# PEER layer on one Trainium2 core: 64 of 256 tokens by gathered rows, 192 by dense products

## The chip, the core and the metric

The kernel runs on one core of a Trainium2 chip. The core has five engines that run their own instruction queues in order: TensorE for matrix products (in the profile PE, its weight loads apart as PEld), VectorE (DVE), ScalarE (ACT), GpSimd (POOL) and SyncE (SP), the last of which here only issues transfers. Transfers run on 16 DMA engines. The metric is the device time in microseconds (us) of one execution; lower is better.

## The reference

A two-layer block over 256 latent tokens and 256 context tokens, D = 1024. Each layer ends in a PEER step: for every token 8 heads choose 16 of 16384 experts each, so 128 experts a token, and every expert has a row in a table u and a row in a table v (1024 numbers each).

```python
def _peer(h, w_query, sub_keys, expert_u, expert_v):
    ...
    idx = jnp.take_along_axis(cand_idx..., pos, axis=-1)      # (token, head, 16)
    gate = jax.nn.softmax(best, axis=-1)
    def retrieve(args):
        hb, ib, gb = args
        act = jax.nn.gelu(jnp.einsum('td,thkd->thk', hb, expert_u[ib]), approximate=False)
        wgt = gb * act
        return jnp.einsum('thk,thkd->td', wgt, expert_v[ib])
    ...
# last layer: only the 256 latent tokens go through _peer, then
x = x + xg2 * _peer(hx, ...)
return rmsnorm(x, final_norm_w)
```

## The kernel before

The kernel is one long program; a scheduler orders each engine's queue when it is compiled. In the last layer PEER is done **dense**, for all 256 tokens at once, in these steps:

- `dense_select`: the normed tokens (transposed, split into two rounded parts `Hh` and `Hl`, so that products in the one-pass type fp32r keep their precision) are scored against the keys; `chosen` holds for each token the two key numbers and the gate of its 128 choices. VectorE does most of it.
- `build`: for every token VectorE makes two one-hot matrices (`two`, one instruction for 4 tokens, and `one`, one for each token), TensorE multiplies them into the token's 128x128 table of gates, ScalarE copies it out, and SP writes it to DRAM (`gd<-gs`), 16 tokens a transfer, 16 transfers.
- `stream`: a loop over the 128 row blocks of the tables, 128 experts each. `first(i)` loads the u block (`w<-in_tab`, 512 KB), splits it into `hu` (ScalarE) and `lu` (VectorE, line 1108), and does 24 products (lines 1118 to 1120): 8 slices of the contraction by three terms, u stationary 128x128, tokens moving, 256 columns; Gelu gives `we`. `second(i)` loads the gates of 8 blocks at a time (`g<-gd`, line 1127) and the v block (`hv`, `lv`), multiplies (line 1133), splits the weights into `wh`, `wl`, and does 12 products (line 1141): 2 token blocks by three terms by 2 halves, the weights stationary, v moving, 512 columns. They add up in the four banks `po`, `po`, `pj`, `pj` over all 128 blocks.
- `first` may run ahead of `second` by `LAG[1]` = 32 blocks. The first `second` needs the gates of all 256 tokens, that is, the end of `build`.
- `residual` scales the sums by a row and adds them to the tokens; then the final norm.

The first layer's context tokens go another way, which the change reuses: `gather_rows.by_choice` fetches for each of 128 choices the rows of u (one token on each partition, 4 KB each, 512 KB a fetch, an indirect DMA that POOL issues), and one VectorE instruction (line 982) makes the 128 dot products; then for each token the 128 rows of v are fetched, and TensorE sums them with weights in 32-column tiles (line 1005). Seven buffers (`ROWS`) hold fetched rows.

Of the kernel before, what the change touches and what calls it, by code (L numbers as in the profile page):

```python
# [8 lines left out]
F32 = mybir.dt.float32  # L9
# [86 lines left out]
def _layout(i):  # L96
# [25 lines left out]
    for l in range(depth):  # L122
        a[f"wmod{l}"] = _tiles(i["w_mod"][l], 512)
        w = i["w_in"][l]
        a[f"win{l}"] = _tiles(w[:, :1536], 256)
        a[f"wba{l}"] = np.ascontiguousarray(w[:, 1536:1552].reshape(KT, 128, 16).transpose(1, 0, 2))
        a[f"wrest{l}"] = _tiles(w[:, 1552:], 512)
        a[f"wout{l}"] = _tiles(i["w_out"][l], 512)
        a[f"wq{l}"] = _tiles(i["w_query"][l], 256)
        k = i["sub_keys"][l].reshape(16, 128, 128)  # L130
        a[f"keys{l}"] = np.ascontiguousarray(k.transpose(2, 0, 1))
        if l < depth - 1:
            a[f"u{l}"], a[f"v{l}"] = i["expert_u"][l], i["expert_v"][l]
# [12 lines left out]
def _body(st, tc, a, out, dbg, until):  # L146
# [16 lines left out]
    def nm(s):  # L163
        n_names[0] += 1
        return f"{s}_{n_names[0]}"
# [879 lines left out]
    AHEAD = 100000  # L1045
    HB = {"u": 2, "v": 2}

    def dense_select(l, s, m, dp, side):
# [15 lines left out]
        for b in range(NB):  # L1064
            p = bank([128, 3, 128], f"c{b}")
            for i in range(3):
                pe.transpose(p[:, i], sel[:, b, i].rearrange("p h k -> p (h k)"), ident)
            act.copy(chosen[:, :, b * 128 : b * 128 + 128], p)
        sp.close()
        return Hh, Hl, chosen  # L1070

    def build(chosen, gdram, side, banks):

        bp = Stage("build", side)
        for tg in range(T // TG):
            gs = bp("gs", [128, NKEYS, TG], 2)
            for t4 in range(0, TG, 4):
                t0 = tg * TG + t4
# [12 lines left out]
            nc.sync.dma_start(gdram[:, tg], gs)  # L1091
        bp.close()

    def stream(l, gdram, Hh, Hl, make_u, make_v, lag, between=()):

        acc = [[bank([128, 512], tag) for _ in range(2)] for tag in ("po", "pj")]
        scores = bank([128, 2, T], "s")
# [15 lines left out]
        def first(i):  # L1113
            hi, lo = table(i, 0, "u", dve.tensor_tensor, make_u)
            p = scores[:, i % 2]
            for k in range(KT):
                ks = slice(k * 128, k * 128 + 128)
                pe.matmul(p, hi[:, ks], Hh[:, k], start=(k == 0), stop=False)  # L1118
                pe.matmul(p, hi[:, ks], Hl[:, k], start=False, stop=False)  # L1119
                pe.matmul(p, lo[:, ks], Hh[:, k], start=False, stop=(k == KT - 1))  # L1120
            w = acts[i] = make_u("we", [128, T], lag + 1)
            act.activation(w, p, AF.Gelu)

        def second(i):
            if i % IG == 0:
                acts["g"] = make_v("g", [128, T // TG, IG, TG], 2)
# [5 lines left out]
            wh = make_v("wh", [128, T], 2, F32R)  # L1132
            dve.tensor_tensor(wt, wt, g, OP.mult)
            act.copy(wh, w)  # L1134
            wl = make_v("wl", [128, T], 2, F32R)
            dve.tensor_tensor(wl, w, wh.bitcast(F32), op=OP.subtract)
            for b in range(NB):
                ts = slice(b * 128, b * 128 + 128)
                for j, (x, y) in enumerate(((wh, hi), (wh, lo), (wl, hi))):
# [13 lines left out]
                second(i - lag)  # L1153
        return acc

    def gdram():
        return dr.tile([128, T // TG, NKEYS, TG], F32, tag="g", name=nm("gd"))


    m = mods[0]  # L1160
# [93 lines left out]
    su = Stage("stream_u", "right")  # L1254
    sw = Stage("split")
    with using(split=sw):
        Hh, Hl, keys = dense_select(1, LAT, m, dp, "right")
    sw.close()
    sv = Stage("stream_v")
    gd = gdram()  # L1260
    build(keys, gd, "right", ("c0", "c1", "c2"))
    residual(1, LAT, m, stream(1, gd, Hh, Hl, su, sv, LAG[1]))
    sv.close()
    su.close()
    dp.close()

# [26 lines left out]
```

## Time and profile before

| | us |
|---|---|
| median of 3 runs | 3301.32 (3293.26 to 3307.34) |
| the profiled execution, its own time | 3294.41 |
| its span, first to last instruction | 3292.7 |
| last layer: `build` runs in | 2495 to 2635 |
| last layer: first product of `second` | 2645.7 |
| last layer: products of `second` end | 3276.4 |

| engine | busy us | share of the span |
|---|---|---|
| PE | 2858.5 | 87% |
| PEld | 2348.9 | 71% |
| DVE | 2207.6 | 67% |
| ACT | 1343.1 | 41% |
| POOL | 860.7 | 26% |

Shares of the whole span mix stages with different limits, so the stages of the last layer are read one by one. Each view of the profile shows what an engine did in a stretch and, in square brackets, how long it had waited and for whom.

### The profile page before, as it was taken

To read this page: it belongs to the slowest core of one execution; us is meant where nothing else is said; L and a number is where in the kernel's file an instruction comes from. 1 tells how busy PE (TensorE), PEld (TensorE's weight loads), DVE (VectorE), ACT (ScalarE), POOL (GpSimd) and SP (SyncE) were. 2 spreads that over 40 slices of the span, in tenths; PEclk is the share of its full clock that TensorE was granted. 3 is DMA by queue.
4 is the path that set the end of the run, shared out by engine and by line. 5 is a ranking of instruction groups with operands and counts; after the bars stand their busy time and mean duration, and the time that the engine had idled before them with its cause. 6 is when DMAs were issued, how large, how long until landed. Compare 5 with 4: busy or idle time off the path is not lost. (4 is left out here: it accounts for less than half of the span.)

```text
span 3292.7 us, 47160 instructions
## 1 busy us (share of the span) xinstructions
PE 2858.5 (87%) x17467; PEld 2348.9 (71%) x17467; DVE 2207.6 (67%) x4920; ACT 1343.1 (41%) x2348; POOL 860.7 (26%) x638
## 2 busy tenths in 40 slices
PE   7998954778897888878789999999779889999998
PEld 4686744645452676767678999868578878889997
DVE  4534587789982688889895655652499955555555
ACT  4432212201251344444455645543335644544443
POOL 0140018985445333333310122134230000000000
PEclk8998976888899989999999999999889999999999
DMA  7622416589899999999985543361234575566663
GB/s 260 212 94 64 153 58 217 181 290 349 311 389 389 343 369 360 367 367 389 383 325 189 172 154 116 92 227 52 95 124 171 201 239 201 199 206 205 213 212 131
DMA packets 246165, 746.52 MB, mean 227 GB/s; under 512 B 21168, under 2 KB 94256, under 8 KB 225456
## 3 DMA queue, kind: packets, MB, share of 16 engines
q1 hardware_dynamic: 190320, 474.54, 41.8%
q0 software_dynamic: 55296, 268.46, 21.8%
q8 instruction: 137, 2.24, 0.3%
q14 instruction: 92, 0.75, 0.1%
q10 hardware_dynamic: 320, 0.52, 0.1%
HBM read 707.27 MB, written 35.65 MB: 226 GB/s over the span
## 5 line engine op out<-in xcount | busy, mean ns | idle before, releaser
L1118 PE MATMUL s<-Hh,hu 128*128 128x256 f32 x2048 | 601.5, 294 | 73.4 <-ACT hu L1107 50.5
L1120 PE MATMUL s<-Hh,lu 128*128 128x256 f32 x2048 | 599.5, 293 | 58.9 <-DVE lu L1108 58.9
L1119 PE MATMUL s<-Hl,hu 128*128 128x256 f32 x2048 | 592.2, 289 | 0.0
L1118 PEld LDWEIGHTS s<-Hh,hu 128*128 128x128 f32 x2048 | 404.7, 198 | 95.7 <-ACT hu L1107 58.2
L1108 DVE TENSOR_TENSOR lu<-w,hu 128x1024 fp32r<-128x1024 f32 x256 | 315.9, 1234 | 228.9 <-ACT hu L1107 228.8
L1120 PEld LDWEIGHTS s<-Hh,lu 128*128 128x128 f32 x2048 | 404.7, 198 | 72.1 <-DVE lu L1108 71.6
L1108 DVE TENSOR_TENSOR lv<-w,hv 128x1024 fp32r<-128x1024 f32 x256 | 314.9, 1230 | 173.3 <-ACT hv L1107 164.3
L1119 PEld LDWEIGHTS s<-Hl,hu 128*128 128x128 f32 x2048 | 405.0, 198 | 8.4
L1107 ACT CAST hu<-w 128x1024 fp32r<-128x1024 f32 x256 | 267.8, 1046 | 330.2 <-PE s L1119 253.0
L1107 ACT CAST hv<-w 128x1024 fp32r<-128x1024 f32 x256 | 267.4, 1044 | 159.8 <-PE pj L1141 116.1
L970 POOL DMA_INDIRECT uv<-in_uv,idx x128 | 206.9, 1616 | 405.1 <-DVE acc L1029 384.7
L982 DVE SCALAR_TENSOR_TENSOR uv<-uv,h 128x1024 f32<-128x1024 f32 x128 | 189.3, 1493 | 45.3 <-DMA uv<-in_u,idx 45.0
L232 POOL TENSOR_TENSOR C<-L,levels 128x512 f32<-128x512 f32 x96 | 137.8, 1446 | 290.4 <-DVE L L645 166.7
L970 POOL DMA_INDIRECT uv<-in_u,idx x128 | 177.6, 1387 | 45.3 <-issue 24.4
L1141 PE MATMUL po<-hv,wh 128*128 128x512 f32 x512 | 164.7, 402 | 14.3 <-ACT wh L1134 13.8
L970 POOL DMA_INDIRECT uv<-in_v,idx_t x128 | 131.1, 1024 | 129.1 <-PE s L1005 103.4
L1141 PE MATMUL po<-lv,wh 128*128 128x512 f32 x512 | 162.7, 399 | 0.1
L1141 PE MATMUL po<-hv,wl 128*128 128x512 f32 x512 | 162.2, 397 | 0.0
L1029 DVE SCALAR_TENSOR_TENSOR acc<-uv,dot,acc 128x1024 f32<-128x1024 f32 x127 | 162.2, 1277 | 0.0
L1141 PE MATMUL pj<-hv,wl 128*128 128x512 f32 x512 | 162.1, 397 | 0.0
L1141 PE MATMUL pj<-lv,wh 128*128 128x512 f32 x512 | 162.1, 396 | 0.0
L1141 PE MATMUL pj<-hv,wh 128*128 128x512 f32 x512 | 161.7, 397 | 0.0
(426 smaller groups left out, 5883.6 us busy)
## 6 DMA issues: line engine op xcount, KB each, us to landing
w<-in_tab SPq DMA_DIRECT2D x512, 512.0 KB, 4.6
w<-in_wmod SPq DMA_DIRECT2D x96, 512.0 KB, 4.7
gd<-gs SPq DMA_DIRECT2D x32, 1024.0 KB, 5.5
g<-gd SPq DMA_DIRECT2D x32, 1024.0 KB, 8.4
w<-in_wq SPq DMA_DIRECT2D x48, 512.0 KB, 4.0
w<-in_win SPq DMA_DIRECT2D x44, 512.0 KB, 4.2
w<-in_wrest SPq DMA_DIRECT2D x24, 512.0 KB, 3.7
w<-in_wout SPq DMA_DIRECT2D x24, 512.0 KB, 4.5
```

Source lines behind the costliest of these rows:

```text
L232: pool.tensor_tensor(out, x, y, op=op)
L970: pool.indirect_dma_start(out=t, out_offset=None, in_=a[f"{table}{l}"], in_offset=bass.IndirectOffsetOnAxis(ap=index, axis=0))
L982: dve.scalar_tensor_tensor(u, u, 1.0, st["h2", b], op0=OP.mult, op1=OP.mult, accum_out=dots[:, j : j + 1])
L1029: dve.scalar_tensor_tensor(acc, uv[:, D:], dot, acc, op0=OP.mult, op1=OP.add)
L1107: act.copy(hi, raw)
L1108: eng(lo, raw, hi.bitcast(F32), op=OP.subtract)
L1118: pe.matmul(p, hi[:, ks], Hh[:, k], start=(k == 0), stop=False)
L1119: pe.matmul(p, hi[:, ks], Hl[:, k], start=False, stop=False)
L1120: pe.matmul(p, lo[:, ks], Hh[:, k], start=False, stop=(k == KT - 1))
L1141: pe.matmul(acc[b][n], x[:, ts], y[:, n * 512 : n * 512 + 512], start=(i == 0 and j == 0), stop=(i == NKEYS - 1 and j == 2),)
```

## The change

In the last layer, tokens 192 to 255 (`FEW` = 64) leave the dense path. `dense_select` makes their expert numbers in two layouts, and their normed rows; the 128 partitions hold 64 tokens twice. `gather_few` does for them what `by_choice` does: 64 fetches of u (choice j of the 64 tokens and choice j + 64), 64 dot products on VectorE, and 64 fetches of v (one token each) with 32 steps of 4 products on TensorE. `build` and `stream` work on 192 tokens. In `second` the product is turned round: v is stationary (8 slices of 128 columns), the weights move (192 columns), 24 products in place of 12, and the sums come out transposed. So after the stream four copies, 16 transposes and two more copies bring them back to token order. In the diff the parts follow one another as they stand in the code: `dense_select`, `gather_few`, `build`, `first`, `second`, and the main part of the last layer.

```diff
+        if rows is not None:
+            ts = slice(T - FEW, T)
+            idx_f = sp("idx_f", [128, FEW])
+            dve.scalar_tensor_tensor(idx_f, chosen[:, 0, ts], float(NKEYS), chosen[:, 1, ts], op0=OP.mult, op1=OP.add)
...
+                pe.matmul(p[cs], idx_f, ident[:, cs], start=True, stop=True)
+            dve.tensor_copy(idx, p)
+            h2 = rows("h2", [128, D])
...
+    def gather_few(l, rows):
...
+        for j in range(FEW):
+            u = fetch("u", few["idx"][:, j : j + 1])
+            dve.scalar_tensor_tensor(u, u, 1.0, few["h2"], op0=OP.mult, op1=OP.mult, accum_out=dots[:, j : j + 1])
...
+        act.activation(w_t, p, AF.Gelu)
+        dve.tensor_tensor(w_t, w_t, few["gate"], OP.mult)
+        dve.tensor_copy(spots_of, w_t.rearrange("p (g r) -> p g r", g=2))
+        p = bank([128, 512], "vb")
+        for r in range(pairs):
+            vs = [fetch("v", few["idx_t"][:, g * pairs + r : g * pairs + r + 1]) for g in range(2)]
+            for n in range(2):
+                for g in range(2):
+                    o = 32 * (2 * n + g)
+                    pe.matmul(
+                        p[o : o + 32], wz[:, g * pairs + r], vs[g][:, n * 512 : n * 512 + 512],
+                        start=(r == 0), stop=(r == pairs - 1), tile_position=(0, o),
+                    )
...
-        for tg in range(T // TG):
+        for tg in range(n // TG):
...
-                pe.matmul(p, hi[:, ks], Hh[:, k], start=(k == 0), stop=False)
+                pe.matmul(p, hi[:, ks], Hh[:, k, 0:n_tok], start=(k == 0), stop=False)
...
+            terms = ((wh, hi), (wh, lo), (wl, hi))
+            if n_tok < T:
+                for k in range(KT):
+                    for j, (x, y) in enumerate(terms):
+                        pe.matmul(
+                            acc[k // 4][k // 2 % 2][:, k % 2 * n_tok : k % 2 * n_tok + n_tok],
+                            y[:, k * 128 : k * 128 + 128], x,
...
-    build(keys, gd, "right", ("c0", "c1", "c2"))
-    residual(1, LAT, m, stream(1, gd, Hh, Hl, su, sv, LAG[1]))
+    build(keys, gd, "right", ("c0", "c1"), n_tok)
+    with using(vb="c2"):
+        y = gather_few(1, rows)
+    sv = Stage("stream_v")
+    sums = stream(1, gd, Hh, Hl, su, sv, LAG[1], n_tok=n_tok)
+    yT = sv("yT", [128, KT, n_tok])
...
+            pe.transpose(ps[k // 4][0:n, k % 4 * 128 : k % 4 * 128 + 128], yT[:, k, b * 128 : b * 128 + n], ident)
...
+    residual(1, LAT, m, halves)
```

The scheduler puts the new work between the old. All queues are as before up to the last layer's selection. VectorE, in the middle of `build`, before: one-hot matrices (`two`, `one`) and the split of u blocks (`lu`).

```order
L1108 TENSOR_TENSOR lu_21794<-w_21791,hu_21793 128x1024
L1081 TENSOR_TENSOR two_20489<-chosen_19040,iota 128x512
L1088 TENSOR_SCALAR one_20491<-iota,chosen_19040 128x128 x4
L1081 TENSOR_TENSOR two_20502<-chosen_19040,iota 128x512
L1088 TENSOR_SCALAR one_20504<-iota,chosen_19040 128x128 x4
L1108 TENSOR_TENSOR lu_21826<-w_21823,hu_21825 128x1024
```

And now, at the same place: the dot products (`uv,dots`, line 1117) stand among them.

```order
L1151 TENSOR_TENSOR two_20504<-chosen_19040,iota 128x512
L1158 TENSOR_SCALAR one_20506<-iota,chosen_19040 128x128 x4
L1117 SCALAR_TENSOR_TENSOR uv_20972,dots_20899<-uv_20972,h_4293_20217 128x1024
L1117 SCALAR_TENSOR_TENSOR uv_20975,dots_20899<-uv_20975,h_4293_20217 128x1024
L1117 SCALAR_TENSOR_TENSOR uv_20978,dots_20899<-uv_20978,h_4293_20217 128x1024
L1117 SCALAR_TENSOR_TENSOR uv_20981,dots_20899<-uv_20981,h_4293_20217 128x1024
L1178 TENSOR_TENSOR lu_22011<-w_22008,hu_22010 128x1024
L1117 SCALAR_TENSOR_TENSOR uv_20984,dots_20899<-uv_20984,h_4293_20217 128x1024
L1151 TENSOR_TENSOR two_20519<-chosen_19040,iota 128x512
```

All 64 dot products stand between the first and the last of the 48 groups (one `two` and four `one`) that `build` now has; 21 `lu` stand there, where 22 stood before among 64 groups.

TensorE, in the stream: the products of a v step (`wz`, line 1132) now stand between those of `first` (lines 1188 to 1190). The product that needs only the first of the step's two fetches stands alone, the three others follow later in a row.

```order
L1188 MATMUL s_21367<-Hh_19035,hu_23068 128x192
L1132 MATMUL c_4524_21099<-uv_21270,wz_20897 32x512
L1132 MATMUL c_4524_21099<-uv_21268,wz_20897 32x512
L1132 MATMUL c_4524_21099<-uv_21270,wz_20897 32x512
L1189 MATMUL s_21367<-Hl_19036,hu_23068 128x192
L1190 MATMUL s_21367<-Hh_19035,lu_23069 128x192
```

Of the 128 products of the v steps 40 (10 steps) stand ahead of the first product of `second`, and 88 (22 steps) behind it, in 43 such runs. Ahead of it stand 34 blocks of `first`, before as now.

TensorE at the end of the stream, before: the last product of `first` stands 24 products ahead of the end of `second`.

```order
L1119 MATMUL s_21086<-Hl_19036,hu_27362 128x256
L1120 MATMUL s_21086<-Hh_19035,lu_27363 128x256
L1141 MATMUL po_21082<-hv_28115,wh_28119 128x512
L1141 MATMUL po_21083<-hv_28115,wh_28119 128x512
L1141 MATMUL po_21082<-lv_28116,wh_28119 128x512
```

And now it stands 337 products, 14 blocks of `second`, ahead of it.

```order
L1189 MATMUL s_21367<-Hl_19036,hu_28783 128x192
L1190 MATMUL s_21367<-Hh_19035,lu_28784 128x192
L1212 MATMUL pj_4594_21366<-wl_29458,hv_29451 128x192
L1212 MATMUL po_21363<-wh_29490,hv_29486 128x192
L1212 MATMUL po_21363<-wh_29490,lv_29487 128x192
```

In these names the operand in front is the one that moves, and the one behind it is stationary.

## Rows read from the trace of the kernel before

**Rows 1.** Windows: length; busy us (instructions) by engine; granted clock, DMA share, GB/s
```profile
2495.00:2635.00 140.00, 128.71 (x1053) 124.46 (x1054) 131.41 (x343) 91.07 (x110) 0.00 (x0) 1.00 0.57 200
2635.00:2646.00 11.00, 0.86 (x6) 0.67 (x6) 1.22 (x4) 1.59 (x4) 0.00 (x0) 0.65 0.79 244
2646.00:3276.00 630.00, 629.35 (x3791) 559.39 (x3791) 356.63 (x472) 299.92 (x439) 0.00 (x0) 1.00 0.61 203
3276.00:3293.00 17.00, 0.41 (x2) 0.00 (x0) 11.88 (x36) 2.30 (x4) 0.00 (x0) 0.62 0.23 93
```
**Rows 2.** Timeline of VectorE in `build`: start, us, engine, line, operation
```profile
2602.00 1.22 DVE L1108 TENSOR_TENSOR lu<-w,hu 128x1024 fp32r<-128x1024 f32 x1
2603.14 0.69 DVE L1081 TENSOR_TENSOR two<-chosen,iota 128x512 f32<-128x512 f32 x1
...
2604.76 0.68 DVE L1081 TENSOR_TENSOR two<-chosen,iota 128x512 f32<-128x512 f32 x1
```
**Rows 3.** Timeline from the end of `build` to the first product of `second`
```profile
2639.17 8.92 SPq L1127 DMA_DIRECT2D g<-gd  x3
2644.78 2.77 DVE L1133 TENSOR_TENSOR we<-we,g 128x256 f32<-128x256 f32 x8 [12.25 <-DMA g<-gd]
...
2645.69 1.22 PE L1141 MATMUL po<-hv,wh 128*128 128x512 f32 x2 [10.14 <-ACT wh L1134]
```
**Rows 4.** Timeline of TensorE in the stream: first product of three neighbouring blocks of products
```profile
2849.78 0.28 PE L1118 MATMUL s<-Hh,hu 128*128 128x256 f32 x1
...
2852.65 0.62 PE L1141 MATMUL po<-hv,wh 128*128 128x512 f32 x2
...
2855.43 0.63 PE L1141 MATMUL po<-hv,wh 128*128 128x512 f32 x2
```
**Rows 5.** Timeline of weight loads and products in runs: start, us of the whole run
```profile
2111.09 0.97 PEld L476 LDWEIGHTS s<-g,same 128*128 128x128 f32 x8
2111.20 0.96 PE L476 MATMUL s<-g,same 128*128 128x8 f32 x8
...
309.65 1.67 PE L256 MATMUL pj<-hT,w 128*128 128x256 f32 x7
```
**Rows 6.** Single loads (shortest/median/longest ns); products of line 256 (busy us, mean ns)
```profile
L1118 PEld LDWEIGHTS s<-Hh,hu x1024: 186/192/338, 2422.4 to 3270.2; 128*128 128x128 f32 x171
...
L1005 PEld LDWEIGHTS s<-uv,wz x512: 105/109/178, 804.8 to 1082.2; 128*32 128x32 f32 x171
...
L256 PE MATMUL pj<-hT,w 128*128 128x256 f32 x448 | 102.0, 383 | 0.1
```
**Rows 7.** Line 982, the dot products of the first layer: two neighbours, and waits (us, times)
```profile
717.24 1.21 DVE L982 SCALAR_TENSOR_TENSOR uv<-uv,h 128x1024 f32<-128x1024 f32 x1
...
718.38 1.21 DVE L982 SCALAR_TENSOR_TENSOR uv<-uv,h 128x1024 f32<-128x1024 f32 x1
...
  DMA uv<-in_u,idx: 45.0, 40
```
**Rows 8.** Timeline of line 1005, v steps of the first layer with nothing beside them
```profile
1035.51 1.06 PE L1005 MATMUL s<-uv,wz 128*32 128x512 f32 x6 [0.49 <-DMA uv<-in_v,idx_t]
1037.05 1.04 PE L1005 MATMUL s<-uv,wz 128*32 128x512 f32 x2 [0.47 <-DMA uv<-in_v,idx_t]
1038.58 1.06 PE L1005 MATMUL s<-uv,wz 128*32 128x512 f32 x6 [0.49 <-DMA uv<-in_v,idx_t]
```
**Rows 9.** Transfers: a window of v fetches alone; landing of fetches; landing of table blocks
```profile
1019.00:1083.00 64.00, 47.27 (x174) 6.26 (x168) 0.00 (x0) 0.00 (x0) 34.66 (x37) 0.94 0.99 374
...
DMA to landing us min/median/max: 4.3/8.1/13.3
...
w<-in_tab SPq DMA_DIRECT2D x198, 512.0 KB, 3.8
```
**Rows 10.** Timeline of the last blocks of the stream and of the end
```profile
3268.01 1.05 ACT L1107 CAST hv<-w 128x1024 fp32r<-128x1024 f32 x1 [1.50 <-PE pj L1141]
...
3269.09 1.23 DVE L1108 TENSOR_TENSOR lv<-w,hv 128x1024 fp32r<-128x1024 f32 x1 [2.13 <-ACT hv L1107]
...
3275.75 0.69 DVE L904 TENSOR_TENSOR upd<-po,row 128x512 f32<-128x512 f32 x1 [3.13 <-PE po L1141]
3275.78 0.63 PE L1141 MATMUL pj<-hv,wl 128*128 128x512 f32 x2
```

More of the change, by code (lines that the diff above doesn't have):

```diff
@@ L1068, in dense_select @@
             act.copy(chosen[:, :, b * 128 : b * 128 + 128], p)
+        if rows is not None:
+            ts = slice(T - FEW, T)
+            idx_f = sp("idx_f", [128, FEW])
+            dve.scalar_tensor_tensor(idx_f, chosen[:, 0, ts], float(NKEYS), chosen[:, 1, ts], op0=OP.mult, op1=OP.add)
+            idx_t = rows("idx_t", [128, FEW], 1, I32)
+            dve.tensor_copy(idx_t, idx_f)
+            idx = rows("idx", [128, FEW], 1, I32)
+            p = bank([128, FEW], "c0")
+            for c in range(2):
+                cs = slice(c * FEW, c * FEW + FEW)
+                pe.matmul(p[cs], idx_f, ident[:, cs], start=True, stop=True)
+            dve.tensor_copy(idx, p)
+            h2 = rows("h2", [128, D])
+            for half in range(2):
+                p = bank([128, 4, 128], f"c{half}")
+                for k in range(4):
+                    for c in range(2):
+                        pe.matmul(
+                            p[c * FEW : c * FEW + FEW, k], hT[:, half * 4 + k, ts], ident, start=True, stop=True
+                        )
+                act.copy(h2[:, half * 512 : half * 512 + 512], p.rearrange("p a b -> p (a b)"))
+            few.update(h2=h2, idx=idx, idx_t=idx_t, gate=chosen[:, 2, ts])
@@ L1069, in dense_select, with fetch @@
         sp.close()
         return Hh, Hl, chosen
-    def build(chosen, gdram, side, banks):
+    FEW = 64
+    few = {}
+    def gather_few(l, rows):
+        pairs = 32
+        y = rows("y", [128, D])
+        wz = rows("wz", [128, FEW, pairs])
+        pool.memset(wz, 0.0)
+        spots_of = wz.rearrange("p (g r) c -> p g (r c)", g=2)[:, :, 0 : pairs * pairs : pairs + 1]
+        def fetch(table, index):
+            t = rows("uv", [128, D], ROWS)
+            pool.indirect_dma_start(
+                out=t, out_offset=None, in_=a[f"{table}{l}"], in_offset=bass.IndirectOffsetOnAxis(ap=index, axis=0)
+            )
+            return t
+        dots = rows("dots", [128, FEW])
+        for j in range(FEW):
+            u = fetch("u", few["idx"][:, j : j + 1])
+            dve.scalar_tensor_tensor(u, u, 1.0, few["h2"], op0=OP.mult, op1=OP.mult, accum_out=dots[:, j : j + 1])
+        p = bank([128, FEW], "vb")
+        for c in range(2):
+            cs = slice(c * FEW, c * FEW + FEW)
+            pe.matmul(p[cs], dots, ident[:, cs], start=True, stop=True)
+        w_t = rows("w_t", [128, FEW])
+        act.activation(w_t, p, AF.Gelu)
[10 more added lines that the diff above has]
+                        start=(r == 0), stop=(r == pairs - 1), tile_position=(0, o),
+                    )
+        o = rows("sum", [128, 512])
+        act.copy(o, p)
+        act.copy(y[FEW:, 512:], o[FEW:])
+        act.dma_start(y[FEW:, 0:512], o[0:FEW])
+        return y
@@ L1256, in _body @@
     with using(split=sw):
-        Hh, Hl, keys = dense_select(1, LAT, m, dp, "right")
+        Hh, Hl, keys = dense_select(1, LAT, m, dp, "right", dp)
     sw.close()
-    sv = Stage("stream_v")
-    gd = gdram()
-    build(keys, gd, "right", ("c0", "c1", "c2"))
-    residual(1, LAT, m, stream(1, gd, Hh, Hl, su, sv, LAG[1]))
+    rows = Stage("rows")
+    n_tok = T - FEW
+    gd = gdram(n_tok)
+    build(keys, gd, "right", ("c0", "c1"), n_tok)
+    with using(vb="c2"):
+        y = gather_few(1, rows)
+    sv = Stage("stream_v")
+    sums = stream(1, gd, Hh, Hl, su, sv, LAG[1], n_tok=n_tok)
+    yT = sv("yT", [128, KT, n_tok])
+    for i in range(4):
+        (act.copy if i % 2 else dve.tensor_copy)(
+            yT[:, 2 * i : 2 * i + 2], sums[i // 2][i % 2][:, 0 : 2 * n_tok].rearrange("p (k t) -> p k t", k=2)
+        )
+    halves = []
+    for b, n in enumerate((128, n_tok - 128)):
+        ps = [bank([128, 512], t) for t in (("c0", "c1"), ("c2", "s"))[b]]
+        for k in range(KT):
+            pe.transpose(ps[k // 4][0:n, k % 4 * 128 : k % 4 * 128 + 128], yT[:, k, b * 128 : b * 128 + n], ident)
+        if b:
+            for i in range(2):
+                act.copy(y[0:n, i * 512 : i * 512 + 512], ps[i][0:n])
+            ps = [y[:, i * 512 : i * 512 + 512] for i in range(2)]
+        halves.append(ps)
+    residual(1, LAT, m, halves)
     sv.close()
+    rows.close()
     su.close()
```

31 lines of the change are left out of this document (18 added, 13 removed).

## The prediction

> **What bounds the kernel now.** The queues are unchanged up to the last layer's selection, so only what follows 2495 us counts. I read the windows by stage first [rows 1]. In `build` VectorE is busy 131.4 of 140 us and TensorE has cover: that stage is VectorE's. Then come 11 us of handing over, the gates going to DRAM and back [rows 3]. From 2646 to 3276 us TensorE is busy 629.35 of 630 us at the full granted clock, 1.00, which is the 2.4 GHz level, with VectorE at 357 and ScalarE at 300 us: that stage is TensorE's alone. The last 17 us are a VectorE chain. So the questions are three: how long `build` keeps VectorE, how long a product takes in the stream, and what else lands on TensorE.
>
> The stream, from rows: 24 products of `first` take from 2849.78 to 2852.65 us, 0.1196 us each; the 12 of `second` from there to 2855.43 us, 0.2317 us each [rows 4]. Behind the first product of `second` stand 94 blocks of `first` and 128 of `second`: 94 x 24 x 0.1196 = 269.8 and 128 x 12 x 0.2317 = 355.9, together 625.7 us, against 630.7 us in the trace (2645.7 to 3276.4); 5 us are waits at the start.
>
> **The change part by part.**
>
> *`build`, and the start of `second`.* A group of 4 tokens costs VectorE 1.62 us (2603.14 to 2604.76) and a `lu` 1.14 us (2602.00 to 2603.14) [rows 2]: 64 x 1.62 + 22 x 1.14 = 129 us, which is the trace's 131. Now 48 groups are 77.8 us and 21 `lu` 23.9 us. The 64 dot products stand between them at 1.14 us each (717.24 to 718.38) [rows 7]: 73.0 us. Index arithmetic, with a wait for TensorE's small product, I put at 3 us. Sum 177.7, some 49 us more than 129. Waits for the fetches come on top: the first layer lost 45.0 us over 128 dot products [rows 7], so 22 us for 64; but there they stood almost without other work, and here a dot product comes every 2.8 us while a fetch arrives every 1.53 us where nothing else moves (1035.51, 1037.05, 1038.58) [rows 8]. Bounds 0 and 22; I take 5. `build` ends 54 us later. The handing over stays [rows 3], so `second` starts at about 2700 us.
>
> A second path leads to the same point: TensorE's queue has 10 v steps, 20 fetches, ahead of the first product of `second`. Weights for them are ready some 6 us before `build` ends (the last dot product stands 8 groups and 3 `lu` ahead, 16.4 us; Gelu, gate and spreading need about 10). Seven fetches are there by then, 13 more at 1.53 us take 20 us, and a last step 1 us. That is 15 us after the end of `build`; the gates take 13. Both ways +54 to +56; I take **+55**, bounds +42 (fetches free, old waits gone too) and +75 (22 us of waits).
>
> *The products of the stream.* 94 x 24 + 128 x 24 = 5328 products, all with 128 stationary columns and 192 moving. No row shows fp32r with fewer than 256 moving columns. Two bounds: by moving columns, the step from 256 to 512 costs (0.2317 - 0.1196) / 256 = 0.438 ns a column [rows 4], so 192 would take 0.0916 us. But each product has its own weight load, and the run of line 476 has only 8 moving columns and still needs (0.97 - 0.19) / 7 = 0.111 us a load [rows 5]. Loads of 32 and of 128 columns differ by 186 - 105 = 81 ns over 96 columns [rows 6], 0.84 ns a column, 108 ns for 128: the load streams, and loads do not overlap one another. So a product cannot come under 0.111 us, and 0.1196 us, today's price with 256 columns, is the upper end: most of today's price of a `first` product is the load, which the change does not shorten, and `second` pays 24 loads in place of 12. I take 0.112: 5328 x 0.112 = 596.7 us, **-29** against 625.7; bounds -34 (0.111) and +12 (0.1196).
>
> The Trainium skill, page "TensorE: Matmul & The Clock Gate", section "LDWEIGHTS (loading the stationary operand)", gives columns / 1.2 in ns, 107 ns for 128; line 476 agrees with its 0.111 us. By it alone the stream would be 570 us. The same page's section "Back-to-back issue gap" gives columns / 2.4 + 2.5 ns, 82.5 ns for 192, and 440 us; that is the first rival below, with its own rows.
>
> *The v steps in the stream.* 22 steps in 43 runs. A plain f32 record with 256 columns follows the last at (1.67 - 0.38) / 6 = 0.215 us [rows 5, 6], with 512 at 0.43; a product is two records, 0.86 us, and the run of two in the first layer took 1.04 us from start to end [rows 8]. Six records in three tiles took 1.06: the tiles run beside each other. So each run costs 0.86 us whether it holds one product or three: 43 x 0.86 = **+37**; bounds +19 (the lone product finds cover) and +45 (1.04 each).
>
> *The end of the stream.* 14 blocks of `second` now stand without `first`, 24 x 0.112 = 2.7 us each. Two buffers for v blocks: a load lands in 3.8 us [rows 9], then `hv` 1.05 and `lv` 1.23 us [rows 10], with handovers 6.4 us for two blocks, 3.2 us a block. 14 x 0.5 = **+7**; bounds 0 and +14.
>
> *The way back.* Before, the first `upd` started 0.7 us ahead of the last product's end (3275.75, 3275.78 + 0.63) [rows 10]. Now two rounds of copies of 384 columns come first, 0.55 us each (0.69 us for 512), then transposes: `upd` starts about 2.7 us after. **+3**; bounds +2 and +5.
>
> *Free.* POOL's 128 issues: it has nothing else to do after selection [rows 1]. Splitting `wh`, `wl` and Gelu get shorter by a quarter on engines that aren't the bound. What waits for POOL is covered: seven buffers are 3.5 steps of some 7 us, 25 us, against 13.3 us for the slowest landing [rows 9].
>
> Sum: 55 - 29 + 37 + 7 + 3 = +73 us. On the profiled execution's 3294.4 us that is 3367; it lies 7 us under the median, so a median would be between 3367 and 3374. **Forecast 3370 us**, own range 3323 (all low ends) to 3442 (all high).
>
> **The rivals.**
>
> *The load hides: moving columns decide.* Then a product costs 0.0916 us [rows 4] and the stream 488 us, -138; the blocks at the end wait 1 us each, +14. 55 - 138 + 37 + 14 + 3 = -29: 3265 us, faster. It decides from 0.098 us a product downwards, where the saving pays the other 101 us. For it: products of 256 columns are near what columns alone would cost. Against it: line 476 [rows 5], and the durations of loads by width [rows 6].
>
> *A narrow fp32r product loses its one pass.* If under 256 columns it ran as plain f32 does, two records of 0.215 x 0.75, it would cost 0.32 us, 5328 of them 1718 us, +1092, and the 34 blocks ahead of `second` would no longer fit under `build` (about +100 instead of +55): near 4530 us. For it: no row shows the opposite. Against it: nothing in the trace shows a price that jumps with width.
>
> *Transfers become the bound.* In `build` 64 u fetches (33.5 MB), 21 table blocks (11 MB), 12 gate transfers (12.6 MB) and 7 v fetches (3.7 MB) are 61 MB in 190 us, 320 GB/s, where 200 flowed before [rows 1] and 374 at a DMA share of 0.99 [rows 9]. In the stream a v step with its block of tables is 2.2 MB in 7.1 us, 310 GB/s. With 270 GB/s `build` takes 35 us more and 22 steps 1 us more each: +57, 3427 us. It decides below 310 GB/s. Against it: the first layer's fetches reached more.
>
> **How the numbers follow.** Forecast 0.74, load hides 0.10, one pass lost 0.06, transfers 0.10. The range 3318 to 3435 takes in the forecast's own range but for its last ends, and the transfers' case, 0.84 less some 0.04. Measurement tells 0.5% (16 us) from no change: faster 0.10 (the first rival), same 0.04 (the forecast's low tail), slower 0.86.
>
> **What would show it.** Right: `build` ends near 2685 us and VectorE is full up to there; `first` and `second` products follow each other at 0.111 to 0.12 us; 43 runs of 0.86 us; TensorE is full in the stream at clock 1.00. Wrong: products at 0.09 us (the saving is real), at 0.3 (the type fails), idle TensorE before `uv` or dot products waiting for `uv` (transfers), or dot products that find room in VectorE's queue so that `second` starts at 2645.

## The result, and the profile after

| | before | after |
|---|---|---|
| median, us | 3297.29 (3291.72 to 3307.34, 4 runs) | 3405.49 (3395.59 to 3407.44, 4 runs) |
| ratio, 95% interval | | 1.0312 (1.0289 to 1.0334) |
| span of the profiled execution, us | 3292.7 | 3393.8 |

The change makes the kernel 3.1% slower. The profiled execution lost 101.1 us. To place them I cut the last layer at four points of the timeline, the same in every kernel: the start of the first `two` of `build`, the start of its last `two`, the start of the first product of `second`, the start of the last one. `build` is the first stretch, the handing over the second, the stream the third, and the end reaches from there to the end of the span.

| us | start of `build` | `build` | handing over | stream | end |
|---|---|---|---|---|---|
| before | 2495.7 | 135.1 | 14.9 | 630.3 | 16.7 |
| after | 2504.6 | 170.9 | 38.2 | 659.2 | 20.9 |
| difference | +8.9 | +35.8 | +23.3 | +28.9 | +4.2 |

The windows of the changed kernel, cut at its own stages, answer to [rows 1]. Columns: window, length, busy us and instructions of PE, PEld, DVE, ACT, POOL, then granted clock, DMA share, GB/s.

```profile
2505.00:2678.00 173.00, 126.57 (x813) 118.62 (x812) 170.91 (x387) 66.58 (x81) 107.48 (x74) 0.81 0.93 334
2678.00:2714.00 36.00, 24.78 (x161) 13.20 (x160) 8.34 (x10) 8.38 (x12) 17.58 (x18) 0.95 1.02 381
2714.00:2858.00 144.00, 141.85 (x942) 100.83 (x945) 55.17 (x94) 39.35 (x62) 39.72 (x37) 0.95 0.87 293
2858.00:3330.00 472.00, 472.00 (x4228) 471.44 (x4222) 259.72 (x350) 224.65 (x353) 0.00 (x0) 1.00 0.67 209
```

In `build` VectorE is full (170.91 of 173). In the next 36 us no engine is, but the transfers are (share 1.02). In the last window TensorE is full, and so are its weight loads: 471.44 of 472, where [rows 1] have 559 of 630.

The handing over, from the timeline, answers to [rows 3]: the last transfer of gates to DRAM, their reading back, the last of the ten v steps that stand ahead of `second` on TensorE, the first use of the gates, the first product.

```profile
2675.45 0.69 DVE L1151 TENSOR_TENSOR two<-chosen,iota 128x512 f32<-128x512 f32 x1
...
2683.75 0.33 SPq L1161 DMA_DIRECT2D gd<-gs  x1
...
2691.74 6.05 SPq L1197 DMA_DIRECT2D g<-gd  x2
...
2705.92 1.06 PE L1132 MATMUL c<-uv,wz 128*32 128x512 f32 x6 [0.49 <-DMA uv<-in_v,idx_t]
...
2712.92 2.24 DVE L1203 TENSOR_TENSOR we<-we,g 128x192 f32<-128x192 f32 x8 [11.33 <-DMA g<-gd]
...
2713.72 0.53 PE L1212 MATMUL po<-wh,hv 128*128 128x192 f32 x1 [6.74 <-ACT wh L1204]
```

The gates leave 8.3 us after the last `two` (4.5 before: 2635.3 after 2630.8 us), the write takes 8 us, and 21 us pass from the issue of the first read to its use, where [rows 3] have 5.6. On TensorE the ten v steps end at 2707.0 us; then it waits 6.7 us for the gates. So by these times `second` could not have started before 2707 even with the gates there: two paths grew, and the gates took only the last 6.7 us.

The pace of the stream, from TensorE's timeline (the end of one block of `second`, the end of the next block of `first`; between the rows lie 24 products):

```profile
3002.80 0.27 PE L1212 MATMUL pj<-wl,hv 128*128 128x192 f32 x1
...
3005.48 0.28 PE L1190 MATMUL s<-Hh,lu 128*128 128x192 f32 x1
```

2.68 us for 24 products is 0.1117 us, and so is the mean from 2858 to 3330 us. [Rows 4] had 0.1196 for 256 columns and 0.2317 for 512.

A run of v steps between two products of `first`:

```profile
2788.45 0.27 PE L1189 MATMUL s<-Hl,hu 128*128 128x192 f32 x1
2788.65 1.05 PE L1132 MATMUL c<-uv,wz 128*32 128x512 f32 x2
2789.63 0.36 PE L1190 MATMUL s<-Hh,lu 128*128 128x192 f32 x1
2789.82 0.27 PE L1188 MATMUL s<-Hh,hu 128*128 128x192 f32 x1
```

One product (two records, x2) takes 1.05 us from start to end; from the product ahead to the second one behind pass 1.37 us, where two distances are 0.22. The distance behind the run, 0.19 us, is wider too.

Added up over all starts in the stream: 5328 x 0.1117 = 595.1 us; 43 places with v steps, 47.2 us more than one ordinary distance at each; 5.9 us at waits that the trace names; 11.3 us of single wider distances without a named wait. Of these 3.7 us stand right behind the 43 runs, 3.2 in the first 7 us, where the granted clock is 0.50, 2.4 in two short stretches behind that have the same distance of 0.21 us, and 1.9 among the last blocks. The sum is 659.5, against 659.2.

### The profile page after: what moved, and what is told of

It reads as the page before. It is cut to its first block, busy times and chain, and to the rows that moved or that the text cites. A ratio compares the mean times of both kernels' runs of the same rounds, so it can differ in the third digit from the quotient of the medians.

```text
span 3393.8 us, 51038 instructions
## 1 busy us (share of the span) xinstructions
PE 2912.8 (86%) x19187; PEld 2417.4 (71%) x19187; DVE 2243.7 (66%) x4975; ACT 1313.7 (39%) x2341; POOL 1027.8 (30%) x767
## 5 line engine op out<-in xcount | busy, mean ns | idle before, releaser
L1188 PE MATMUL s<-Hh,hu 128*128 128x256 f32 (+1 forms) x2048 | 605.8, 296 | 84.1 <-ACT hu L1177 61.0
L1190 PE MATMUL s<-Hh,lu 128*128 128x256 f32 (+1 forms) x2048 | 605.2, 296 | 81.6 <-DVE lu L1178 81.6
L1189 PE MATMUL s<-Hl,hu 128*128 128x256 f32 (+1 forms) x2048 | 596.0, 291 | 0.0
L1189 PEld LDWEIGHTS s<-Hl,hu 128*128 128x128 f32 x2048 | 418.2, 204 | 10.9 <-issue 6.7
L1178 DVE TENSOR_TENSOR lv<-w,hv 128x1024 fp32r<-128x1024 f32 x256 | 314.5, 1231 | 101.1 <-ACT hv L1177 88.1
L982 DVE SCALAR_TENSOR_TENSOR uv<-uv,h 128x1024 f32<-128x1024 f32 x128 | 194.0, 1532 | 41.1 <-DMA uv<-in_u,idx 40.6
L1192 ACT ACTIVATE we<-s 128x256 f32<-128x256 f32 (+1 forms) x256 | 90.8, 355 | 222.9 <-PE s L1190 221.0
L1204 ACT CAST wh<-we 128x256 fp32r<-128x256 f32 (+1 forms) x256 | 96.5, 377 | 183.3 <-PE pj L1212 110.3
L1159 PEld LDWEIGHTS c<-one,two 128*128 128x128 f32 x896 | 115.8, 203 | 62.3 <-issue 31.8
L1021 DVE SCALAR_TENSOR_TENSOR uv<-uv,h 128x1024 f32<-128x1024 f32 x128 | 156.2, 1221 | 5.0 <-DMA uv<-in_uv,idx 5.0
L1005 PE MATMUL s<-uv,wz 128*32 128x512 f32 x512 | 123.3, 657 | 32.0 <-DMA uv<-in_v,idx_t 30.2
L1206 DVE TENSOR_TENSOR wl<-we,wh 128x256 fp32r<-128x256 f32 (+1 forms) x256 | 101.5, 397 | 73.7 <-ACT wh L1204 68.9
## 6 DMA issues: line engine op xcount, KB each, us to landing
g<-gd SPq DMA_DIRECT2D x16, 1024.0 KB, 16.7
```

The costliest lines, as they stand in the source:

```text
L982: dve.scalar_tensor_tensor(u, u, 1.0, st["h2", b], op0=OP.mult, op1=OP.mult, accum_out=dots[:, j : j + 1])
L1005: pe.matmul(p[o : o + 32], wz[:, g * pairs + r], vs[g][:, n * 512 : n * 512 + 512], start=(r == 0), stop=(r == pairs - 1), tile_position=( ...
L1021: dve.scalar_tensor_tensor(uv[:, 0:D], uv[:, 0:D], 1.0, st["h2", b], op0=OP.mult, op1=OP.mult, accum_out=dot)
L1178: eng(lo, raw, hi.bitcast(F32), op=OP.subtract)
L1188: pe.matmul(p, hi[:, ks], Hh[:, k, 0:n_tok], start=(k == 0), stop=False)
L1189: pe.matmul(p, hi[:, ks], Hl[:, k, 0:n_tok], start=False, stop=False)
```

## Experiments

All stage times below are taken as in the table above; "before" is timed beside each kernel on the same chip. The theory: the dense part for 192 tokens gains little because every product pays for its own weight load, and the gathered work costs VectorE's time in `build`, TensorE's time in the stream, and, what I had not foreseen, the handing over.

### Without the gathered way

```diff
-        Hh, Hl, keys = dense_select(1, LAT, m, dp, "right", dp)
+        Hh, Hl, keys = dense_select(1, LAT, m, dp, "right")
...
-        y = gather_few(1, rows)
+    y = rows("y", [128, D])
+    pool.memset(y, 0.0)
```

> The changed kernel without the gathered way: tokens 192 to 255 get no expert sum at all (zeros), so neither index arithmetic, fetches, dot products nor v steps are there; build, stream and the way back work on 192 tokens as changed. My theory (every product pays its own weight load, the gathered work costs the rest): build about 110 us instead of 136.8 before (48 groups and 22 lu), handing over 13 us, 5328 products at 0.111 us and the lone blocks at the end +6, so the stream is about 28 us shorter than before, the end +4: about 3297 - 26 - 28 + 4 = 3247 us. Rival 'moving columns decide': 0.0916 us a product, about 3145 us. Rival 'the dense part for 192 tokens is itself the loss': 3297 or more.

Measured: 3262.98 us, ratio 0.9863 (0.9829 to 0.9898). `build` 110.0, handing over 14.7, stream 603.2, end 20.7 us. The three differences are those that were expected (-25, -27, +4). The total is 16 us above my figure, and its profiled execution reached `build` at 2516.3 us, 20 us later than before, through work that is the same. So the dense part alone is a gain of 36 to 45 us (by the medians, by the ratio), and the gathered work loses some 140.

### What a product costs: columns moved or columns loaded

Three kernels, all without the gathered way. In the first two, the products move 64 or 128 of the 192 columns; in the third they load 64 of the 128 stationary columns. `second` is changed in the same way.

```diff
-                pe.matmul(p, hi[:, ks], Hh[:, k, 0:n_tok], start=(k == 0), stop=False)
+                c = slice(0, n_tok if n_tok == T or i < 2 else NARROW)
+                pe.matmul(p[:, c], hi[:, ks], Hh[:, k, c], start=(k == 0), stop=False)
...
```

```diff
+                h = 128 if n_tok == T or i < 2 else 64
+                ks = slice(k * 128, k * 128 + h)
-                pe.matmul(p, hi[:, ks], Hh[:, k, 0:n_tok], start=(k == 0), stop=False)
+                pe.matmul(p[0:h], hi[:, ks], Hh[:, k, 0:n_tok], start=(k == 0), stop=False)
...
```

> As the run without the gathered way, and all products of the stream but those of the first two blocks of the first kind and the first and last block of the second kind move only 64 of the 192 token columns, so the sums of the other columns are left out. Stationary width (128 columns) and number of products are the same. My theory (load-bound): the pace stays at 0.111 us, the time stays within 10 us of the run without the gathered way. Rival 'moving columns decide': 0.036 us a product, the stream falls under 350 us, where transfers would hold it, about 2950 us in all. Rival 'a narrow fp32r product loses its one pass': several times slower.

> As the run with 64 moving columns, but 128 of the 192 (the sums of the other 64 columns are left out). With 64 the granted clock fell to 0.50 for the whole stream and a product took 0.213 us, so that run did not tell load from columns at the full clock. Theory (load-bound): where the clock is 1.00 a product takes 0.111 us, as with 192 columns, and the time is that of the run without the gathered way, about 3263 us, plus what a fallen clock adds. Rival 'moving columns decide' (0.0885 us for 192 columns with half a load, 0.44 ns a column): 0.06 us a product, about 3000 us.

> As the run without the gathered way, and all products of the stream but those of the same few blocks load only 64 of the 128 stationary columns, so half of the scores and half of the output rows are left out. Moving columns (192) and number of products are the same. My theory (load-bound): a load costs half, some 0.055 us, and the pace falls to the price of 192 moving columns, between 0.083 and 0.092 us: the stream loses 100 to 150 us, the time is 100 us or more under the run without the gathered way. Rival 'each fp32r product has a floor of 0.111 us whatever it loads': no change.

Measured: 64 columns 3797.56 us, 128 columns 3790.14 us, both over 500 us above the run they were cut from; half the load 3168.49 us, ratio 0.9586 (0.9548 to 0.9624), 94 us under it. No theory expected the first two. First 64 columns, a window from 2800 us and two neighbouring products of TensorE's timeline; then the same of 128 columns, from 2900 us:

```profile
2800.00:2900.00 100.00, 100.00 (x470) 100.00 (x470) 29.47 (x39) 24.44 (x38) 0.00 (x0) 0.50 0.38 112
```

```profile
2860.11 0.40 PE L1215 MATMUL po<-wl,hv 128*128 128x64 f32 x1
2860.32 0.40 PE L1215 MATMUL po<-wh,hv 128*128 128x64 f32 x1
```

```profile
2900.00:3000.00 100.00, 100.00 (x471) 100.00 (x470) 30.24 (x40) 24.50 (x38) 0.00 (x0) 0.50 0.37 110
```

```profile
2860.17 0.41 PE L1215 MATMUL pj<-wh,lv 128*128 128x128 f32 x1
2860.39 0.41 PE L1215 MATMUL pj<-wl,hv 128*128 128x128 f32 x1
```

The granted clock stands at 0.50, the 1.2 GHz level, with TensorE and its loads busy all the time. So these runs say nothing of the total that was asked for, but of the price they say much: 100 us hold 470 products, 0.213 us each, with 64 columns as with 128. The changed kernel itself has the third point, 192 columns in the first us of its stream, where its clock is 0.50 too:

```profile
2714.26 0.41 PE L1212 MATMUL po<-wh,hv 128*128 128x192 f32 x1
2714.47 0.41 PE L1212 MATMUL po<-wh,lv 128*128 128x192 f32 x1
2714.69 0.41 PE L1212 MATMUL pj<-wh,hv 128*128 128x192 f32 x1
```

Again 0.21 us. At this level the price does not depend on the moving columns at all. The price at the full clock stands in the two runs too, in shorter stretches: first 64 columns, at the start of the stream, then 128 columns, in `build` (window, two neighbours).

```profile
2641.45:2643.60 2.15, 2.15 (x22) 2.15 (x21) 1.12 (x4) 1.30 (x2) 0.00 (x0) 1.00 0.94 273
2642.73 0.28 PE L1190 MATMUL s<-Hh,hu 128*128 128x64 f32 x1
2642.84 0.28 PE L1191 MATMUL s<-Hl,hu 128*128 128x64 f32 x1
```

```profile
2609.67:2611.91 2.24, 2.24 (x23) 2.24 (x22) 2.24 (x6) 1.07 (x1) 0.00 (x0) 1.00 0.90 282
2609.78 0.28 PE L1191 MATMUL s<-Hl,hu 128*128 128x128 f32 x1
2609.89 0.28 PE L1192 MATMUL s<-Hh,lu 128*128 128x128 f32 x1
```

That is 0.11 us with 64 and with 128 columns. The six unbroken runs of 20 or more products at this clock with 64 columns, and the seven with 128, have 0.110 to 0.113 us on average, where 192 columns have 0.112. So the load-bound price holds at both levels, and the rival's 0.036 and 0.06 us are out. In the 64-column run the clock fell at 2644 us, behind 24 such products, with TensorE busy throughout; why it then stayed at 0.50 is not shown. With half the load, in a window with a clock of 0.98, it falls (timeline of TensorE):

```profile
2901.07 0.25 PE L1191 MATMUL s<-Hl,hu 128*64 128x192 f32 x1
2901.16 0.25 PE L1192 MATMUL s<-Hh,lu 128*64 128x192 f32 x1
2901.25 0.25 PE L1190 MATMUL s<-Hh,hu 128*64 128x192 f32 x1
```

0.09 us, 0.089 from 2900.10 to 2901.96 us (21 products). So 192 moving columns cost 0.089 us where 64 columns are loaded, and 0.112 where 128 are: the load decides (half the load also means half the output rows, which this run does not separate from it), and the quarter of the tokens that left the stream was already paid for by it. The rival with 0.0916 us a product had nearly the right price for the columns, and the wrong one for the product. The stream of this run took 524.2 us, 79 less than without the gathered way and not the 119 that the price alone would give (5328 x 0.0224), as TensorE now waits for others, 26 us of it for `hv` and `lv`; most of the rest of the 94 us lies ahead of the stream. One reading has to be given up here:

```profile
2900.00:3000.00 100.00, 94.67 (x1036) 93.23 (x1034) 60.99 (x85) 53.20 (x85) 0.00 (x0) 0.98 0.76 239
```

With half the load PEld is recorded as busy nearly as long as PE as well, so that share does not tell whether the load or the columns set the price.

### Turned round with all 256 tokens

The kernel before with only `second` turned round, and the way back.

```diff
-    n_tok = T - FEW
+    n_tok = T
...
-            if n_tok < T:
+            if turned:
```

> The kernel before with one thing changed: in the last layer the second products have v stationary (24 products of 256 moving columns instead of 12 of 512), with the way back by copies and transposes; all 256 tokens dense, nothing gathered. My theory: 24 x 0.1196 = 2.87 us a block instead of 12 x 0.2317 = 2.78, 128 blocks: +11 us; the end +4; about 3297 + 15 = 3312 us. Rival 'turning costs nothing, a product is paid by its columns': about 3301 us. Rival 'the turned form has waits of its own in the stream, at its start or end': 3325 us or more.

Measured: 3316.75 us, ratio 1.0043 (1.0024 to 1.0061). Stream 636.8 (+6.5), end 21.0 us (+4.3), `build` 137.7, handing over 14.3. A product took 0.1187 us, a little under the 0.1196 of `first` before, so +6.5 in place of +11. Turning costs what its 24 loads cost; it has no waits of its own. From here to 192 tokens the stream gains 636.8 - 603.2 = 33.6 us, all that 64 tokens fewer are worth there.

### Without the v phase, and with half the u fetches

```diff
-        p = bank([128, 512], "vb")
-        for r in range(pairs):
-            vs = [fetch("v", few["idx_t"][:, g * pairs + r : g * pairs + r + 1]) for g in range(2)]
...
+        pool.memset(y, 0.0)
```

> The changed kernel with the u fetches, dot products, Gelu and gates of the 64 gathered tokens, but without their v phase: no v fetches, no v steps on TensorE, their expert sums are zeros. My theory (the v steps cost about 59 us in the stream and push the last gate transfers late): build stays at about 172 us, the handing over falls from 36.6 us to about 13, the stream from 659.5 to about 603: 3405 - 23 - 56 = about 3326 us. Rival 'the handing over is late because of the u fetches, the split of the stages or the narrower gates': it stays at about 36 us, time about 3350. Rival 'the v steps hide behind other waits': time stays above 3380.

Measured: 3330.66 us, ratio 1.0088 (1.0061 to 1.0115). `build` 176.7, handing over 18.7, stream 602.7 us: the v phase is worth 19.5 us of the 23.3 in the handing over and 56.5 in the stream. The handing over of this kernel, in the lines that stand above for the changed one:

```profile
2688.72 0.69 DVE L1138 TENSOR_TENSOR two<-chosen,iota 128x512 f32<-128x512 f32 x1
...
2696.46 0.33 SPq L1148 DMA_DIRECT2D gd<-gs  x1
...
2701.32 1.43 SPq L1184 DMA_DIRECT2D g<-gd  x2
...
2706.52 2.24 DVE L1190 TENSOR_TENSOR we<-we,g 128x192 f32<-128x192 f32 x8 [1.55 <-DMA g<-gd]
```

The last transfer is issued 7.7 us after the last `two`, nearly as late as in the changed kernel (8.3), so products of v steps ahead of `build`'s last ones on TensorE are not the point. The write takes 4.9 us in place of 8, and the read 5.2 in place of 21: the gates were slow beside the v fetches, 18 of which fall into the 36 us from 2678 on. But this kernel also lacks the ten v steps ahead of `second`, which in the changed kernel held TensorE until 2707 us, so it does not show what faster gates alone would be worth.

```diff
-            u = fetch("u", few["idx"][:, j : j + 1])
+            if j % 2 == 0:
+                u = fetch("u", few["idx"][:, j : j + 1])
```

> The changed kernel with every second u fetch left out: two dot products in a row use the same fetched rows (so the weights of the gathered tokens are wrong in half their choices), 64 dot products on VectorE as before, 16.8 MB less of transfers in build. My theory (VectorE holds build, the fetches are covered): build stays at about 172 us, the time within 10 us of the changed kernel, unless the v fetches, which may now start earlier, move the handing over. Rival 'the transfers hold build': 45 us less at 374 GB/s, build about 130 us, time about 3360 us.

Measured: 3404.67 us, ratio 1.0326 (1.0298 to 1.0355). `build` 175.7 us at a DMA share of 0.71, where the changed kernel had 0.93:

```profile
2521.00:2698.00 177.00, 127.29 (x847) 117.17 (x842) 171.22 (x385) 65.91 (x82) 71.19 (x47) 0.81 0.71 245
```

VectorE is just as full (171.22 of 177). The transfers don't hold `build`; the dot products do.

### The v steps in longer runs

```diff
-                for g in range(2):
+                for g in (1, 0):
                     o = 32 * (2 * n + g)
```

> The changed kernel with one edit: of the two rows a v step waits for, TensorE asks for the later one first, so that the four products of a step stand together in its queue: 23 runs in the stream instead of 43, with the same products. My theory (every run of the plain f32 products costs about 1.15 us whether it holds one product or four): about 20 x 1.15 = 23 us less, about 3382 us. Rival 'the price goes with the products, or TensorE waits for the later row': no change, 3400 or more.

Measured: 3386.98 us, ratio 1.0282 (1.0258 to 1.0306). The intervals of this ratio and of the changed kernel's meet, so the totals alone would be a weak proof; the stages are not: `build` 170.0 and the handing over 37.9 us as in the changed kernel, the stream 636.5 in place of 659.2 us, -22.7 for 20 runs fewer, 1.13 us each. A run of four products:

```profile
2780.62 1.06 PE L1132 MATMUL c<-uv,wz 128*32 128x512 f32 x8
2781.62 0.36 PE L1212 MATMUL po<-wh,lv 128*128 128x192 f32 x1
```

Four products (x8) take 1.06 us, where one alone took 1.05.

### The gathered way moved into the stream

All the gathered work is put behind the first blocks of the stream, where VectorE has room, first at once, then spread, then spread with the fetches ahead of their use. All three have the longer runs of the kernel above.

```diff
+        zero = rows("zero", [128, 1])
+        dve.tensor_scalar(zero, few["we"][:, 0:1], 0.0, None, op0=OP.mult)
+        idx = rows("idx_i", [128, FEW], 1, I32)
+        dve.tensor_scalar(idx, few["idx"], zero, None, op0=OP.add)
...
-    sums = stream(1, gd, Hh, Hl, su, sv, LAG[1], n_tok=n_tok)
+    sums = stream(1, gd, Hh, Hl, su, sv, LAG[1], {40: late}, n_tok=n_tok)
...
```

> The changed kernel with the v runs joined and the whole gathered way put behind block 36 of the first products (a zero made from that block's weights is added to the indices, so nothing of it can start earlier): fetches, dot products and v steps all stand in the stream, build and the handing over are free of them. The same result is computed. My theory: as the run without the gathered way (3247 us by my estimate) plus 32 runs of 1.15 us = 37 us and 4 us of index work ahead of build: about 3288 us. VectorE has room in the stream (357 us busy of 630 before, 73 us of dot products come). Rival 'the dot products wait for their fetches in VectorE's queue and hold up lu and lv, so that TensorE waits': 3330 us or more. Rival 'transfers': 183 MB in 630 us, 290 GB/s, over 374 only if they bunch; 3320 us.

Measured: 3372.61 us, ratio 1.0217 (1.0192 to 1.0243). `build` (108.7) and handing over (14.4) are free, as expected, but the stream takes 711.5 us, 108 more than without the gathered work, where 37 were expected. My theory fell. Four windows of its stream:

```profile
2630.00:2700.00 70.00, 54.33 (x433) 53.84 (x434) 45.81 (x92) 21.87 (x36) 22.52 (x16) 0.85 0.91 313
2700.00:2800.00 100.00, 84.99 (x567) 82.20 (x566) 84.01 (x134) 31.19 (x48) 59.00 (x44) 0.80 1.00 375
2800.00:2900.00 100.00, 93.15 (x718) 79.36 (x716) 51.86 (x76) 32.53 (x51) 42.95 (x38) 0.91 0.95 343
2900.00:3000.00 100.00, 97.23 (x804) 78.76 (x803) 43.23 (x56) 38.01 (x58) 35.90 (x33) 0.98 0.94 338
```

The transfers are full, TensorE has gaps and, with them, a lower granted clock. From the starts of its products: 37 us at the 32 places with v steps, as expected, 38 us at waits of TensorE for `hu`, `lu`, `hv` and `lv`, and 42 us of wider distances, most of them 0.21 us, the pace at a clock of 0.50. That is 117, and the run without the gathered way has 8 of these. That the full transfers make the gaps is so far an argument. So the next kernel spreads the work.

```diff
+            if j % 2 == 0:
+                t = after_now("idx")(slice(j, j + 2))
+            u = fetch("u", t[:, j % 2 : j % 2 + 1])
...
+    steps = {36 + i: step(2 - (i % 3 > 0)) for i in range(48)}
+    steps.update({87 + 2 * i: step(1) for i in range(32)})
...
```

> The run with the gathered way behind block 36 took 3372.6 us; in its stream the DMA share stood at 0.91 to 1.00 for the 370 us in which the fetches were made and TensorE lost some 41 us there, beside a lower granted clock. Here the same gathered work is spread: from block 36 on four u fetches with their dot products in three blocks, from block 87 on one v step in two blocks, each tied to the newest block's weights (as a zero added to its index) so that it cannot start earlier. The same result is computed. Theory 'the transfers, bunched, held the stream': with about 344 GB/s beside the u part and 311 GB/s beside the v part TensorE does not wait; the time is that of the run without the gathered way (3263) plus 32 runs of 1.14 us, about 3300 us, as before the change. Rival 'the dot products and v steps themselves cost it, wherever they stand (VectorE's queue holds up lu and lv)': 3340 us or more with a DMA share under 0.95.

Measured: 3454.53 us, ratio 1.0468 (1.044 to 1.0495): worse still, with a DMA share of 0.78 to 0.85 in the u part. VectorE's and TensorE's largest waits for rows (us, times, longest), and VectorE's timeline:

```profile
DVE uv L1126 <- DMA uv<-in_u,idx: 99.5, 36, 7.1
PE c L1143 <- DMA uv<-in_v,idx_t: 47.8, 20, 5.0
```

```profile
2874.82 1.23 DVE L1126 SCALAR_TENSOR_TENSOR uv<-uv,h 128x1024 f32<-128x1024 f32 x1 [6.72 <-DMA uv<-in_u,idx]
...
2877.44 1.22 DVE L1126 SCALAR_TENSOR_TENSOR uv<-uv,h 128x1024 f32<-128x1024 f32 x1
...
2878.58 1.23 DVE L1190 TENSOR_TENSOR lv<-w,hv 128x1024 fp32r<-128x1024 f32 x1
```

Dot products wait for a fetch that was released only a moment before, and `lv`, which TensorE needs, stands behind them in VectorE's queue: TensorE waits 37.7 us for `lv`. It waits even longer, 47.8 us, for the rows of its own v steps, which are released as late. VectorE's part is the rival, and both are a fault of my tie, so the last kernel lets six fetches run ahead, and three v steps.

```diff
+            while len(got) < min(j + 6, FEW):
+                c = len(got)
+                if c % 2 == 0:
+                    t = after_now("idx")(slice(c, c + 2))
+                got.append(fetch("u", t[:, c % 2 : c % 2 + 1]))
+            u = got[j]
...
```

> As the spread run (3454.5 us), where VectorE stood 99.5 us before dot products whose rows had not landed, each fetch being released only just before its dot product, and TensorE then waited for lv. Here six rows are fetched ahead of the dot product that uses them, and three v steps ahead; pace and results are the same. Theory 'the late release of the fetches held VectorE's queue, and through lv TensorE': the waits of VectorE for uv fall under 20 us, TensorE is full, the time is the run without the gathered way (3263) plus 32 runs of 1.14 us, about 3300 us. Rival 'interleaving itself costs it (each fetch slows the transfers of w, so hu, lu and lv are late whatever the lead)': 3340 us or more, with TensorE waiting for lu and lv while uv is there.

Measured: 3335.31 us, ratio 1.0102 (1.0082 to 1.0122): 119 us better for the lead alone, and 70 better than the changed kernel, but 35 above my figure. Of VectorE's list of waits the line for `uv`, and TensorE's two largest for rows and `lv`:

```profile
DVE uv L1130 <- DMA uv<-in_u,idx: 25.0, 18, 4.6
```

```profile
PE po L1233 <- DVE lv L1198: 9.1, 13, 3.4
PE c L1151 <- DMA uv<-in_v,idx_t: 8.0, 9, 2.1
```

The stream takes 674.7 us, 71.5 more than without gathered work. From the starts of its products: 47 us at the 33 places with v steps (8 of them waiting for rows, so 1.18 us a run), 13 us more of named waits, 11 us more of wider distances. Both theories had a part: the lead took most of the loss away, and some 24 us of disturbance stay; their cause was not tested. No version here that does the gathered work beats the kernel before: the dense part alone gains 36 to 45 us, and 33 runs of v steps at 1.18 us already take 39.

## Why the prediction was right, point by point

The forecast was 3370 us in 3318 to 3435, slower with a chance of 0.86; 3405 lies within. The rivals did not occur as they were put: products did not follow the columns, no narrow product took the 0.32 us of a lost pass, and the transfers did not hold `build`, though they did set the handing over. But of the 101 us that were lost, 73 had been forecast, and the terms were off in both directions: `build` came out 15 us cheaper and the handing over 23 us dearer. The start of `second` moved by 68 us where +55 with bounds +42 and +75 stood, so that the term held is in part luck. (The high ends of the own range add up to 3445, not 3442.)

- **Start.** `build` began 8.9 us later, where I had 3 for the index chain. The runs without any index chain began between 2503.7 and 2516.3 us, so part of it is a difference between executions; how much stays open.
- **`build`.** Forecast 46 us of work and 5 of waits, measured +35.8. The durations were right: 174.7 us by my sum, 170.9 and a last group of 1.6 in the trace; and half the fetches made no difference. What was wrong are the waits: the trace has 0.7 us for `uv` in place of my 5, and the 8 us that `build` had before (136.7 us with its last group, 129 of them work) are gone, which I had only in the low bound.
- **The handing over.** This is the step that failed: "The handing over stays". It grew by 23.3 us. My second path counted v steps on TensorE and compared them with an unchanged 13 us for the gates; that the v fetches themselves would slow the gates was not in it, though I had worked out 320 GB/s for the stretch before. Without the v phase the read of the gates takes 5.2 us, with it 21. The second path was mis-sized as well: its 15 us behind the end of `build` were 30 (2677.1 to 2707.0). The eighth fetch had to wait for the first v step to free a buffer, was issued at 2674.61 us and used at 2683.37; from there the rows came 1.88 us apart up to the twentieth, in place of 1.53. So even with gates at 13 us the forecast start of `second` would have been too early.
- **The products.** -29 forecast with 0.112 us a product; 0.1117 and 595.1 us, -31. The argument from line 476 [rows 5] was right, and the runs with 64 and 128 columns, at both clocks, and the one with half the load show the load itself. The Trainium skill's page "TensorE: Matmul & The Clock Gate", section "Back-to-back issue gap", gives a formula that makes 82.5 ns of 192 columns, and says itself that it is the gap of an isolated product and counts too little at few columns, for want of the load. The run with half the load comes near that with 89 ns, no product with a full load here does.
- **The v steps.** 43 runs was right, the price was not: 0.86 us forecast, 47.2 / 43 = 1.10 us measured, +47 in place of +37, and 1.18 us, +51, with the wider distance behind each run. I had taken the time of the two records alone, though the bound of 1.04 us [rows 8] stood beside it; what makes up the rest was not tested. The Trainium skill's page "TensorEngine Tiling (Array Packing)", section "Key Properties", says that a change of tiling mode drains the engine, without a price; that a run of one and a run of four take 1.05 and 1.06 us and cost 1.1 to 1.2 us in the stream fits that, and does not prove it.
- **Start of the stream.** 3.2 us of wider distances in its first 7 us at a granted clock of 0.50, and 2.4 in two later stretches at the same distance, were not in the sum. TensorE had been idle for 6.7 us ahead of the first.
- **The end.** Tail +7 forecast, +5.4 measured (337 products in 43.0 us, 37.6 at 0.1117); way back +3, measured +4.2.

The own sum of the measured terms: 8.9 + 35.8 + 23.3 + 28.9 + 4.2 = 101.1.

## What to carry to other kernels

Before taking columns away from a product, see whether its weight load or its columns set the distance to the next one, by changing one of them alone: the busy share of PEld does not tell (471 of 472 us with a full load, 93 of 95 with half). When work moves into an empty resource, price the transfers that it adds against the small transfers that everything waits for, here the gates. A fetch that is tied to its consumer must be released several fetches ahead, or the consumer's in-order queue stops with it.

## What the runs showed of the hardware that was not expected

- With 64 or 128 moving columns in place of 192 the granted clock was 0.50 in all of the stream but some 4 us, with TensorE and its loads recorded as busy 100 of 100 us; with 192 columns, the same instructions otherwise, it was 1.00. The kernels became over 500 us slower by moving less. Why is open.
- At that level a product with 128 loaded columns takes 0.213 us with 64, 128 and 192 moving columns; at 1.00, 0.112 with 64, 128 and 192, and 0.119 with 256; with 64 loaded columns 0.089 with 192.
- A read of gates took 21 us beside v fetches, with 381 GB/s for all transfers together, and 5.2 us without them.
